# Where the modulation products of a two-block transformer stand in TensorE's order, and which tokens its first mixer takes first

## The chip, the cores and the metric

The kernel runs on one core of one Trainium2 chip, in one launch. The metric is the device time of that launch in microseconds (us). Three timed runs of the kernel before took 2777.68, 2779.40 and 2786.29 us; their median is 2779.4 us. The profiled execution is a run of its own.

The engines have short names in the rows: PE is TensorE (PEld its weight loads), DVE is VectorE, ACT is ScalarE, POOL is GpSimd and SP is SyncE, which issues most of the loads from HBM.

## What is computed

A first block of two layers (each a hybrid of sparse attention and a state space model, then a gated feed-forward) works on 256 tokens `x` of width 1024. A second block of two layers takes these as latent tokens together with 256 context tokens. Its layers are modulated: a conditioning vector is multiplied with `w_ada`, and the six resulting rows per layer shift, scale and gate the tokens. Cut to what matters here:

```python
def second_block(x, c, ctx, c_ctx, w_ada, b_ada, ...):      # x is the first block's normed output
    x_lat, x_ctx = x, ctx
    silu_c, silu_cc = jax.nn.silu(c), jax.nn.silu(c_ctx)
    for l in range(DEPTH):                                  # DEPTH = 2
        mod_l = (silu_c @ w_ada[l] + b_ada[l])              # w_ada[l]: 1024 x 6144, float32
        mod_c = (silu_cc @ w_ada[l] + b_ada[l])
        sh1, sc1, g1, sh2, sc2, g2 = jnp.split(mod_l, 6, axis=-1)
        h_l = rmsnorm(x_lat, norm_mix[l]) * (1 + sc1) + sh1
        h_c = rmsnorm(x_ctx, norm_mix[l]) * (1 + sc1c) + sh1c
        o_c, o_l = mixer(h_c, h_l, ...)                     # projections, attention, output projection
        x_lat = x_lat + g1 * o_l
        ...                                                 # sh2, sc2, g2: router and experts
```

`w_ada` depends on nothing that the first block computes, so its products may stand anywhere before the rows that they give are read.

## The kernel before

**Weights.** A float32 weight matrix is streamed in tiles of 128 x 4 x 512 into a ring of four slots (`g.ring`, one tile is 1 MB). `wtiles` (line 140) loads a tile on SP, splits each half of it into a high part (ScalarE, line 158) and a low part (VectorE, line 159), and the users (`lin_a`, `lin_a4`, `lin_b` and others) make three matmuls of each: high by high, high by low, low by high. `lin_a4` (line 181) keeps the split tiles and uses them for two groups of token tiles, one group after the other; `HALVES` is tiles 0 and 1 (latent), then 2 and 3 (context).

**Modulation units.** `ada_units` (line 923) is a generator. Each `next` of it, called through `g.filler`, makes one unit: one load of 1 MB of `w_ada` into a ring slot (line 945) and the products of it into the one PSUM bank `adaps` (line 947). Eight units make a group, six groups (two layers by three) make 48 units. At the end of a group VectorE adds the bias out of the bank (line 951), for two groups of three also a factor (line 955), GpSimd writes the rows to `g.mod` in HBM (line 957), and the next group begins with a bias load on SP into a tile with one buffer (line 941).

Units are drawn in these places:

- `wtiles` draws one at every eighth weight tile (`g.count % 8`, line 152). A layer of the first block takes 88 tiles, the mixer 14.
- `burst(g, n)` (line 307) draws n, each of whose matmuls must stand behind the last product so far (`g.last`). There are bursts of 3 and 4 in each layer of the first block (ahead of its two norms), of 5 at the start of the first mixer, and of 48 in the router, which takes what is left.

**The seam.** The first block ends with `final_norm` (line 800) of `x`, after the last tile of `ffn_w_down` (lines 174 to 176). The first mixer, `mixer_ab` (line 1158), then modulates all four token tiles in `mod_all` (line 1011): root mean square (line 982), two VectorE instructions per tile (lines 993 and 994), transposes and splits (`transpose_split`, lines 1005 to 1008). The context tokens `xc` were loaded after layer 0. The tiles `mh` that hold a modulated token tile have two buffers. Three `lin_a4` follow (lines 1249 to 1251), whose results go through norms and rotary products (`ev_x`, `ev_y`, `ev_z`), then low-rank products, then `attend` (line 1030): for each of eight pairs of heads scores, softmax, transposes and, in `values` (line 1079), the value products. The output projection and the router come behind it.

**What sets the order.** Each engine takes its instructions in an order that is fixed ahead of the run by a planner, which goes by the order of the program and by estimated times; an instruction that is not ready holds up what stands behind it on its engine. SP's order is fixed in the same way, over all loads.

Of the kernel before, what the change touches and what calls it, by code (L numbers as in the profile page):

```python
# [139 lines left out]
def wtiles(g, w2d, ktiles, pieces):  # L140

    nc = g.nc
    n = sum(p[1] for p in pieces)
    for k0 in range(0, ktiles, 4):
        kk = min(4, ktiles - k0)
        t = g.ring.tile([P, 4, 512], F32, name="wraw", tag="wraw")
        at = 0
        for c0, w in pieces:
            nc.sync.dma_start(t[:, :kk, at:at + w], w2d[k0 * P:(k0 + kk) * P, c0:c0 + w].rearrange("(k p) n -> p k n", p=P))
            at += w  # L150
        g.count += 1
        if g.count % 8 == 0:
            g.filler()
        for j in range(0, kk, 2):
            jj = min(2, kk - j)
            hi = g.split.tile([P, 2, 512], F32R, name="whi", tag="whi")
            lo = g.split.tile([P, 2, 512], F32R, name="wlo", tag="wlo")
            nc.scalar.copy(hi[:, :jj, :n], t[:, j:j + jj, :n])  # L158
            nc.vector.tensor_tensor(lo[:, :jj, :n], t[:, j:j + jj, :n], hi[:, :jj, :n].bitcast(F32), op=OP.subtract)  # L159
            yield k0 + j, jj, hi, lo  # L160
# [146 lines left out]
def burst(g, n):  # L307

    if g.last is None:
        for _ in range(n):  # L310
            g.filler()
        return
    with g.tc.issue_after(g.last.ins):
        for _ in range(n):
            g.filler()
# [516 lines left out]
Q_LORA, KV_LORA = 384, 256  # L832
HALVES = (range(2), range(2, 4))
O2_KR, O2_GQ, O2_GK, O2_GV = 640, 672, 1184, 1312
# [152 lines left out]
def modulated(g, pool, rows, tiles, rs=None):  # L987

    nc = g.nc
    rs = rs or rms_all(g, pool, tiles)  # L990
    for (r, y), (x, m) in zip(rs, tiles):
        a, b = rows[m]
        nc.vector.scalar_tensor_tensor(y, x, r, a, op0=OP.mult, op1=OP.mult)
        nc.vector.tensor_tensor(y, y, b, op=OP.add)
        yield y
# [12 lines left out]
        nc.vector.tensor_tensor(xl[:, k0:k0 + kk, t * P:(t + 1) * P], ps[:, :kk], a.bitcast(F32), op=OP.subtract)  # L1008


def mod_all(g, pool, l, xt, xh, xl):
    for i in (0, 2):
        for t, y in enumerate(modulated(g, pool, g.rows, xt[i:i + 2])):
            transpose_split(g, y, 8, xh, xl, i + t)

# [14 lines left out]
def attend(g, pool, pairs, qtiles):  # L1030


    nc = g.nc
    nt = len(qtiles)
    units = [(i, e, j) for i in range(len(pairs)) for e in range(2) for j in range(nt)]
    probs, pts, ready, biases = {}, {}, [], {}
    groups = []
    for j, (t, s0, ns) in enumerate(qtiles):
        if groups and groups[-1][2:] == [s0, ns]:
            groups[-1][1] = j + 1  # L1040
        else:
            groups.append([j, j + 1, s0, ns])

    def fetch(u):
        i, e, j = u
        if pairs[i][5] is not None:
            biases[u] = pairs[i][5](e, qtiles[j][0])

    def front(u):
        i, e, j = u  # L1050
        t, s0, ns = qtiles[j]
        n = ns * P
        ps = g.acc.tile([P, 512], F32, name="accps", tag="acc")
        nc.tensor.matmul(ps[:, :n], pairs[i][0](e, t), pairs[i][1](e, s0 * P, n), start=True, stop=True)
        if u in biases:
            nc.vector.tensor_tensor(ps[:, :S], ps[:, :S], biases.pop(u), op=OP.add)
        mx = pool.tile([P, 1], F32, name="smx", tag="smx", bufs=6)
        sm = pool.tile([P, 1], F32, name="ssm", tag="ssm", bufs=6)
        p = pool.tile([P, 512], F32, name="smp", tag="smp", bufs=5)
        nc.vector.tensor_reduce(mx, ps[:, :n], axis=AX.X, op=OP.max, negate=True)  # L1060
        nc.scalar.activation(p[:, :n], ps[:, :n], AF.Exp, bias=mx, accum_out=sm)
        nc.vector.reciprocal(sm, sm)
        nc.vector.tensor_scalar(p[:, :n], p[:, :n], sm, None, op0=OP.mult)
        probs[u] = p

    def back(u):
        i, e, j = u
        t, s0, ns = qtiles[j]
        if j == 0:
            pts[i, e] = pool.tile([P, 4, nt * P], F32, name="apT", tag="apT", bufs=3)  # L1070
        p, pT = probs.pop(u), pts[i, e]
        pt = g.aux.tile([P, 4, P], F32, name="auxps", tag="aux")
        for s_ in range(ns):
            nc.tensor.transpose(pt[:, s_, :], p[:, s_ * P:(s_ + 1) * P], g.ident)
        nc.scalar.copy(pT[:, s0:s0 + ns, j * P:(j + 1) * P], pt[:, :ns])
        if e == 1 and j == nt - 1:
            ready.append(i)

    def values(i):
        vf, o_hi, o_lo = pairs[i][2:5]  # L1080
        po = g.aux.tile([P, 512], F32, name="auxps", tag="aux")
        for j0, j1, s0, ns in groups:
            for s_ in range(s0, s0 + ns):
                for e in range(2):
                    nc.tensor.matmul(po[64 * e:64 * e + 64, j0 * P:j1 * P], vf(e, s_), pts[i, e][:, s_, j0 * P:j1 * P],
                                     start=(s_ == s0), stop=(s_ == s0 + ns - 1))
        nc.scalar.copy(o_hi, po[:, :nt * P])
        nc.vector.tensor_tensor(o_lo, po[:, :nt * P], o_hi.bitcast(F32), op=OP.subtract)

    lag, early = 3, 4  # L1090
    for u in units[:early]:
        fetch(u)
    for k in range(len(units) + lag + 1):
        if k + early < len(units):
            fetch(units[k + early])
        if k < len(units):
            front(units[k])
        todo = ready[:]
        ready.clear()
        if lag <= k < len(units) + lag:  # L1100
            back(units[k - lag])
        for i in todo:
            values(i)


def out_proj(g, pool, l, oh, ol, w2d, xt):
# [51 lines left out]
def mixer_ab(g, xt):  # L1158
    nc, tc, h = g.nc, g.tc, g.h
    with ExitStack() as st:  # L1160
# [11 lines left out]
        w_in = h["ab_w_in"]  # L1172
        with ExitStack() as s1:
# [7 lines left out]
            with ExitStack() as s2:  # L1181
                p2 = s2.enter_context(tc.tile_pool(name="mab2", bufs=1, side="right"))
                xh = p2.tile([P, 8, 512], F32R, name="mxh")
                xl = p2.tile([P, 8, 512], F32R, name="mxl")
                with tc.tile_pool(name="mabn", bufs=1) as pn:
                    burst(g, 5)
                    mod_all(g, pn, 0, xt, xh, xl)
                p3 = s2.enter_context(tc.tile_pool(name="mab3", bufs=1))
                qnr = p3.tile([P, Q_LORA], F32, name="qnr")
                knr = p3.tile([P, KV_LORA], F32, name="knr")  # L1190
# [55 lines left out]
                        nc.tensor.transpose(pt[:, j, :], v[:, 2 * j:2 * j + 2].rearrange("p a d -> p (a d)"), g.ident)  # L1246
                    nc.scalar.activation(qbT[:, :, t * P:(t + 1) * P], pt, AF.Copy, scale=0.125)

                lin_a4(g, xh, xl, w_in, 8, [(0, Q_LORA), (O2_GK, 128)], HALVES, ev_x)
                lin_a4(g, xh, xl, w_in, 8, [(Q_LORA, KV_LORA), (O2_GV, 128), (O2_KR, 32)], HALVES, ev_y)  # L1250
                lin_a4(g, xh, xl, w_in, 8, [(O2_GQ, 512)], HALVES, ev_z)
            pq = right.enter_context(tc.tile_pool(name="mabq", bufs=1, side="right"))
            qT = pq.tile([P, 8, 512], F32, name="qT2")
            kT = pq.tile([P, 8, 512], F32, name="kT2")
# [626 lines left out]
```

## Time and profile before

| | us |
|---|---|
| median of 3 runs | 2779.4 |
| profiled execution, time | 2780.57 |
| its span | 2778.8 |
| TensorE busy in the span | 2604.0 (94%) |
| VectorE busy | 1542.2 (55%) |
| ScalarE busy | 1024.1 (37%) |
| first block | 0 to about 1203 |
| first mixer, up to its attention | about 1203 to 1320 |
| its attention | about 1320 to 1430 |

A row of the order of instructions gives start, duration, engine, line, operation, tile written, tile read and count; in brackets stands the idle time of the engine just before it and what ended that. Matmuls overlap, so the price of one is read from start to start. A multiplication of float32 operands shows as two records.

### The profile page before, as it was taken

To read this page: it belongs to the slowest core of one execution; us is meant where nothing else is said; L and a number is where in the kernel's file an instruction comes from. 1 tells how busy PE (TensorE), PEld (TensorE's weight loads), DVE (VectorE), ACT (ScalarE), POOL (GpSimd) and SP (SyncE) were. 2 spreads that over 40 slices of the span, in tenths; PEclk is the share of its full clock that TensorE was granted. 3 is DMA by queue.
4 is the path that set the end of the run, shared out by engine and by line. 5 is a ranking of instruction groups with operands and counts; after the bars stand their busy time and mean duration, and the time that the engine had idled before them with its cause. 6 is when DMAs were issued, how large, how long until landed. Compare 5 with 4: busy or idle time off the path is not lost. (4 is left out here: it accounts for less than half of the span.)

```text
span 2778.8 us, 39439 instructions
## 1 busy us (share of the span) xinstructions
PE 2604.0 (94%) x15773; PEld 1840.4 (66%) x15773; DVE 1542.2 (55%) x2878; ACT 1024.1 (37%) x1809; POOL 131.0 (5%) x172
## 2 busy tenths in 40 slices
PE   7999999999999999988997999999989989998897
PEld 5889889977899889867665455445458554333332
DVE  6767768857777668655655434334363654222223
ACT  4556546634566456533652111111122441111011
POOL 0000000000000000011002000000000420000000
PEclk9999999999999999999997999999989889999999
DMA  6544457675455486662133999999933258999996
GB/s 220 196 152 152 150 201 234 202 240 179 136 175 171 150 287 193 203 208 68 54 153 124 402 420 420 420 420 419 385 122 112 92 209 346 420 420 420 420 420 284
DMA packets 207434, 694.56 MB, mean 250 GB/s; under 512 B 18160, under 2 KB 67760, under 8 KB 151184
## 3 DMA queue, kind: packets, MB, share of 16 engines
q1 hardware_dynamic: 201424, 674.18, 64.3%
q0 software_dynamic: 5824, 17.82, 2.0%
q8 instruction: 126, 2.06, 0.3%
q14 instruction: 60, 0.49, 0.1%
HBM read 690.80 MB, written 1.15 MB: 249 GB/s over the span
## 5 line engine op out<-in xcount | busy, mean ns | idle before, releaser
L159 DVE TENSOR_TENSOR wlo<-wraw,whi 128x1024 fp32r<-128x1024 f32 (+1 forms) x406 | 484.9, 1200 | 219.3 <-ACT whi L158 210.5
L158 ACT CAST whi<-wraw 128x1024 fp32r<-128x1024 f32 (+1 forms) x406 | 418.0, 1035 | 392.0 <-PE accps L245 195.4
L1657 PE MATMUL accps<-wraw,xg 128*64 128x512 f32 x2080 | 489.0, 595 | 40.8 <-DMA wraw<-in_moe_w_up 25.6
L1657 PEld LDWEIGHTS accps<-wraw,xg 128*64 128x64 f32 x2080 | 165.2, 138 | 354.6 <-issue 259.5
L244 PE MATMUL accps<-xh,whi 128*128 128x256 f32 x896 | 257.4, 287 | 0.0
L246 PE MATMUL accps<-xh,wlo 128*128 128x256 f32 x896 | 255.0, 285 | 0.0
L245 PE MATMUL accps<-xl,whi 128*128 128x256 f32 x896 | 254.6, 284 | 0.0
L1670 PE MATMUL accps<-wraw,eaT 128*64 128x512 f32 (+1 forms) x1040 | 234.2, 595 | 1.5 <-ACT eaT L1558 1.5
L1539 DVE TENSOR_TENSOR cmt<-auxps,g2r 128x512 f32<-128x512 f32 x108 | 73.6, 688 | 263.8 <-PE auxps L1537 263.2
L244 PE MATMUL accps<-fxh,whi 128*128 128x256 f32 x704 | 200.6, 285 | 0.8 <-ACT whi L158 0.8
L246 PE MATMUL accps<-fxh,wlo 128*128 128x256 f32 x704 | 199.6, 284 | 0.7 <-DVE wlo L159 0.5
L245 PE MATMUL accps<-fxl,whi 128*128 128x256 f32 x704 | 199.8, 284 | 0.0
L244 PEld LDWEIGHTS accps<-xh,whi 128*128 128x128 f32 x896 | 169.6, 189 | 7.7 <-issue 7.4
L246 PEld LDWEIGHTS accps<-xh,wlo 128*128 128x128 f32 x896 | 169.7, 189 | 1.1 <-issue 1.0
L245 PEld LDWEIGHTS accps<-xl,whi 128*128 128x128 f32 x896 | 169.5, 189 | 1.2 <-issue 1.0
L1558 ACT COPY eaT<-auxps 128x512 f32<-128x512 f32 x33 | 19.4, 586 | 408.7 <-PE auxps L1557 408.7
L1670 PEld LDWEIGHTS accps<-wraw,eaT 128*64 128x64 f32 (+1 forms) x1040 | 74.6, 137 | 133.2 <-issue 129.3
L244 PEld LDWEIGHTS accps<-fxh,whi 128*128 128x128 f32 x704 | 135.6, 193 | 6.3 <-issue 4.2
L246 PEld LDWEIGHTS accps<-fxh,wlo 128*128 128x128 f32 x704 | 135.5, 193 | 1.2 <-DVE wlo L159 1.2
L245 PEld LDWEIGHTS accps<-fxl,whi 128*128 128x128 f32 x704 | 135.8, 193 | 0.0
L1567 DVE TENSOR_TENSOR yl<-accps,yh 128x512 fp32r<-128x512 f32 x66 | 45.6, 692 | 161.3 <-ACT yh L1566 161.1
L1566 ACT CAST yh<-accps 128x512 fp32r<-128x512 f32 x66 | 38.6, 585 | 201.7 <-PE accps L1670 201.7
(496 smaller groups left out, 5139.2 us busy)
## 6 DMA issues: line engine op xcount, KB each, us to landing
wraw<-in_moe_w_gate SPq DMA_DIRECT2D x130, 1024.0 KB, 17.3
wraw<-in_moe_w_up SPq DMA_DIRECT2D x130, 1024.0 KB, 17.3
wraw<-in_moe_w_down SPq DMA_DIRECT2D x130, 1024.0 KB, 15.3
wraw<-in_w_in SPq DMA_DIRECT2D x72, 1024.0 KB, 5.1
wraw<-in_w_ada SPq DMA_DIRECT2D x48, 1024.0 KB, 4.9
wraw<-in_ffn_w_up SPq DMA_DIRECT2D x88, 512.0 KB, 5.0
wraw<-in_ffn_w_down SPq DMA_DIRECT2D x20, 1024.0 KB, 5.3
wraw<-in_w_proj_ssd SPq DMA_DIRECT2D x16, 1024.0 KB, 5.1
```

Source lines behind the costliest of these rows:

```text
L158: nc.scalar.copy(hi[:, :jj, :n], t[:, j:j + jj, :n])
L159: nc.vector.tensor_tensor(lo[:, :jj, :n], t[:, j:j + jj, :n], hi[:, :jj, :n].bitcast(F32), op=OP.subtract)
L244: nc.tensor.matmul(o, wh, a, start=(K == 0 and f % per == 0), stop=False, skip_group_check=True)
L245: nc.tensor.matmul(o, wh, b, start=False, stop=False, skip_group_check=True)
L246: nc.tensor.matmul(o, wl, a, start=False, stop=last, skip_group_check=True)
L1539: nc.vector.tensor_tensor(tm, ps, g2r[m][:, sl], op=OP.mult)
L1558: nc.scalar.copy(aT, ps)
L1566: nc.scalar.copy(yh[:, sl], psd[c])
L1567: nc.vector.tensor_tensor(yl[:, sl], psd[c], yh[:, sl].bitcast(F32), op=OP.subtract)
L1657: nc.tensor.matmul(pp[rows], xg[kh][:, k, cols], wt[:, k], start=(K == 0), stop=(K == 7))
L1670: nc.tensor.matmul(psd[c][rows], aT[:, k, rows], wt[:, 2 * kk + c], start=(k == 0), stop=(k == 3))
```

## The change

Four edits:

- `wtiles` draws a unit at every 20th weight tile instead of every eighth.
- `mod_all` takes the order of the token pairs as an argument, and the first mixer gives (2, 0): context tiles first, then latent tiles. The three `lin_a4` of the projections take the halves in reversed order, context first.
- A burst of two units stands behind each of these three projections.
- In `attend`, a unit is drawn after the value products of each pair (the second layer's mixer calls the same function, when no unit is left).

```diff
@@ wtiles
         g.count += 1
-        if g.count % 8 == 0:
+        if g.count % 20 == 0:
             g.filler()
@@
-def mod_all(g, pool, l, xt, xh, xl):
-    for i in (0, 2):
+def mod_all(g, pool, l, xt, xh, xl, first=(0, 2)):
+    for i in first:
         for t, y in enumerate(modulated(g, pool, g.rows, xt[i:i + 2])):
             transpose_split(g, y, 8, xh, xl, i + t)
@@ attend
         for i in todo:
             values(i)
+            g.filler()
@@ mixer_ab
                     burst(g, 5)
-                    mod_all(g, pn, 0, xt, xh, xl)
+
+                    mod_all(g, pn, 0, xt, xh, xl, (2, 0))
@@ mixer_ab
-                lin_a4(g, xh, xl, w_in, 8, [(0, Q_LORA), (O2_GK, 128)], HALVES, ev_x)
-                lin_a4(g, xh, xl, w_in, 8, [(Q_LORA, KV_LORA), (O2_GV, 128), (O2_KR, 32)], HALVES, ev_y)
-                lin_a4(g, xh, xl, w_in, 8, [(O2_GQ, 512)], HALVES, ev_z)
+                lin_a4(g, xh, xl, w_in, 8, [(0, Q_LORA), (O2_GK, 128)], HALVES[::-1], ev_x)
+                burst(g, 2)
+                lin_a4(g, xh, xl, w_in, 8, [(Q_LORA, KV_LORA), (O2_GV, 128), (O2_KR, 32)], HALVES[::-1], ev_y)
+                burst(g, 2)
+                lin_a4(g, xh, xl, w_in, 8, [(O2_GQ, 512)], HALVES[::-1], ev_z)
+                burst(g, 2)
```

## Rows read from the trace of the kernel before

**Rows 1.** The page: the span, and the loads of the modulation weights

```profile
span 2778.8 us, 39439 instructions
...
wraw<-in_w_ada SPq DMA_DIRECT2D x48, 1024.0 KB, 4.9
```

**Rows 2.** Stages: us; busy PE, PEld, DVE, ACT, POOL; clock; DMA share; GB/s

```profile
425.00:600.00 175.00, 175.00 (x1253) 163.08 (x1252) 135.89 (x228) 99.99 (x148) 1.76 (x3) 1.00 0.67 214
...
1203.00:1260.00 57.00, 42.61 (x220) 32.24 (x220) 40.05 (x82) 23.60 (x44) 14.79 (x22) 0.88 0.59 189
1260.00:1320.00 60.00, 53.08 (x250) 43.02 (x249) 31.96 (x70) 22.09 (x36) 9.54 (x8) 0.97 0.20 63
1320.00:1430.00 110.00, 109.33 (x579) 64.90 (x579) 72.76 (x207) 75.60 (x207) 3.64 (x6) 1.00 0.13 45
1212.00:1224.00 12.00, 6.46 (x23) 5.42 (x24) 9.96 (x12) 8.06 (x12) 1.00 (x3) 0.50 0.92 299
```

**Rows 3.** TensorE in order of time, a unit in the first block's stream

```profile
422.59 0.28 PE L245 MATMUL accps<-fxl,whi 128*128 128x256 f32 x1
422.71 0.28 PE L246 MATMUL accps<-fxh,wlo 128*128 128x256 f32 x1
422.92 1.06 PE L947 MATMUL adaps<-wraw,ccs 128*32 128x512 f32 x8
...
424.14 0.28 PE L245 MATMUL accps<-fxl,whi 128*128 128x256 f32 x1
```

**Rows 4.** TensorE in order of time, a burst of four in layer 0

```profile
406.69 3.64 PE L947 MATMUL adaps<-wraw,ccs 128*32 128x512 f32 x32
410.26 0.44 PE L292 MATMUL auxps<-cst,xn 128*128 128x128 f32 x2
```

**Rows 5.** TensorE in order of time, the start of the first mixer

```profile
1203.15 3.64 PE L947 MATMUL adaps<-wraw,ccs 128*32 128x512 f32 x32
1209.56 1.07 PE L947 MATMUL adaps<-wraw,ccs 128*32 128x512 f32 x8 [2.77 <-DVE badat L951]
1216.15 2.79 PE L1005 MATMUL auxps<-cst,mh 128*128 128x128 f32 x12 [5.53 <-DVE mh L994]
1220.33 0.77 PE L199 MATMUL accps<-whi,mxh 128*128 128x512 f32 x1 [1.39 <-ACT mxh L1007]
...
1234.48 0.39 PE L200 MATMUL accps<-wlo,mxh 128*128 128x512 f32 x1
1234.71 0.39 PE L201 MATMUL accps<-whi,mxl 128*128 128x512 f32 x1
```

**Rows 6.** VectorE, then ScalarE in order of time, at the same place

```profile
1207.62 1.28 DVE L808 SCALAR_TENSOR_TENSOR x<-x,fr,fnw 128x1024 f32<-128x1024 f32 x1 [0.66 <-POOL fr L130]
...
1212.39 2.48 DVE L993 SCALAR_TENSOR_TENSOR mh<-x,mr,ma 128x1024 f32<-128x1024 f32 x2 [2.12 <-POOL mr L130]
1214.78 2.35 DVE L994 TENSOR_TENSOR mh<-mh,mb 128x1024 f32<-128x1024 f32 x2
...
1212.26 1.99 ACT L158 CAST whi<-wraw 128x1024 fp32r<-128x1024 f32 x2 [2.17 <-DMA wraw<-in_ab_w_in]
1217.71 1.99 ACT L158 CAST whi<-wraw 128x1024 fp32r<-128x1024 f32 x2 [3.46 <-DMA wraw<-in_ab_w_in]
```

**Rows 7.** TensorE's waits by releaser, 1203 to 1320: us in all, times, longest

```profile
PE auxps L1246 <- DVE hnv L1214: 3.1, 2, 1.7
PE auxps L1226 <- DVE kdup L1223: 2.9, 2, 1.8
...
PE auxps L1246 <- DVE hnv L1027: 2.5, 1, 2.5
```

**Rows 8.** SP: a wait by releaser (us, times, longest), and issues in order

```profile
SPq L941 <- DMA mod<-badat: 8.6, 1, 8.6
...
1205.13 4.40 SPq L149 DMA_DIRECT2D wraw<-in_ab_w_in  x5
```

**Rows 9.** TensorE in order of time, a pair's value products in the attention

```profile
1406.40 2.81 PE L1085 MATMUL auxps<-apT,vb 128*64 128x256 f32 x24
```

## The prediction

> **What bounds the kernel now.** I read the busy time of the engines by stage first [rows 2], since a mean over the span says nothing of one stage. In the first block's stream TensorE is busy for 175.00 of 175 us: it alone sets the pace, VectorE (135.89) and ScalarE (99.99) have slack, and the DMA share is 0.67. In the attention of the first mixer TensorE is busy for 109.33 of 110 us at full clock, with a DMA share of 0.13. Between the two lies the only slack the change can use: TensorE is busy for 42.61 of 57 us and then for 53.08 of 60 us, so 21.3 us are idle. The order of TensorE's instructions shows where [rows 5]: 2.77, 5.53 and 1.39 us at the start of the mixer, before the first product of the projections at 1220.33; the waits by releaser show the longest of the rest, 3.1, 2.9 and 2.5 us for results of VectorE that are to be transposed [rows 7]. Everything that the change touches is therefore priced in TensorE time: full price where it has no idle time, less where it has.
>
> **The modulation unit.** A unit is one load of 1 MB into a slot of the weight ring and eight matmul records. The load lands in 4.9 us [rows 1] and hides behind other work in a saturated stage. On TensorE, single in the stream, the start-to-start step of the neighbours is 0.12 us (422.59 to 422.71); from 422.71 to 424.14 lie two such steps and a unit, so the unit costs 1.43 - 0.24 = 1.19 us [rows 3]. Four in a bunch take from 406.69 to 410.26, so 0.89 us each [rows 4].
>
> **Counting.** Each layer of the first block draws 88 weight tiles, the mixer 14. Before, 176/8 = 22 units stand in the first block's stream, 14 in its four bursts, 5 in the burst at the mixer's start, 1 in the mixer's stream (tile 184), 6 in the router: 48. After, 176/20 = 8 stand in the stream, 14 and 5 as before, 1 in the mixer's stream (tile 180), 6 in the three new pairs, 8 in the attention, 6 in the router. So 14 leave the stream, 6 go behind the projections and 8 into the attention. The router's number does not change, in spite of the title.
>
> **1. Removed from the stream: -16.7 us.** 14 x 1.19. The stream has no idle time that could swallow it, and their 14 loads go from a queue that is not the bound.
>
> **2. Added to the attention: +8.8 us.** There is no wait to fill (109.33 of 110), so each of the 8 is paid in full: between 8 x 0.89 = 7.1 and 8 x 1.19 = 9.5. I take 1.1 each, nearer to the single one, since each stands alone behind a pair's value products [rows 9]. Those products are themselves 64-column tiles, so the switch may be a little cheaper than in the stream. The switch is what makes a single unit dearer than a bunched one: 0.30 us by rows 3 and 4. The Trainium skill (TensorEngine Tiling, Key Properties) says that changing the tiling mode drains TensorE, which speaks against spreading units singly; by that rule all 8 cost 1.19 and the term is 9.5, and by the bunched row it would be 7.1.
>
> **3. Six units behind the projections: +2.7 us.** In pairs they cost 6 x 0.89 = 5.3 us if nothing hides them. They stand behind the last product of a projection, where the transposes of the norms wait, and the three longest kinds of such waits sum to 8.5 us [rows 7]. But these waits come a few products later, in an order fixed ahead of the run, so a unit that runs earlier may only push the wait back. Ends 0 and 5.3; I take the middle. The single one in the mixer's stream is the same before and after.
>
> **4. Context tokens first: -7 us.** Before, TensorE goes idle at 1206.7, when four units are done, because the chain of the latent tokens starts only with the final norm: two products of 1.28 us (L808, the second from 1207.62 to 1208.9), squares and roots, then from 1212.39 on 2.48 and 2.35 us of modulation on VectorE [rows 6], and the first transpose at 1216.15 [rows 5]. The context tokens need none of the final norm; they need room that the last products of the first block hold until about 1203.2. If their modulation runs ahead of the final norm's products, their first transposes come at about 1203.2 + 3.5 (squares and roots, as from 1208.9 to 1212.39) + 2.48 + half of 2.35 = 1210.4; if behind them, at 1208.9 + 2.48 + 1.2 = 1212.6. From the first transpose to the first product it takes 4.2 us before (1216.15 to 1220.33), less at full clock. The weights are the other limit: the first tile's cast starts at 1212.26, on its landing, and takes half of 1.99 [rows 6]. So products start at 1213.3 at best and at 1216.8 at worst, against 1220.33: a gain of 3.5 to 7.0. The second weight tile is cast from 1217.71 [rows 6]; the 24 products on the first tile at 0.23 us (1234.48 to 1234.71) [rows 5] take 5.5 us, so TensorE comes to it at 1218.8 and hardly waits. The latent tokens then have 11 us of context products as cover for their own norm and modulation. What is late next: VectorE, 40.05 busy of 57 [rows 2], which splits weights, modulates and subtracts for both halves at once. With that comes the clock: from 1212 to 1224 the granted clock is 0.50 (1.2 GHz) after the idle 5.53 us, and TensorE's 6.46 us of work there would have taken half at 2.4 GHz [rows 2], so 0 to 3.2 us come back. I take 5.5 and 1.5. The Trainium skill (TensorE: Matmul & The Clock Gate, Part 1) says that the clock falls after an idle TensorE and returns with sustained work; the row agrees. By that rule, if the context transposes break up the idle time, the whole 3.2 comes back and the term is -8.7; if not, -5.5.
>
> **5. The unit count shifts the group ends: +1.3 us.** After every eighth unit VectorE adds the bias out of the one PSUM bank, and the ninth unit waits for it, as it does for 2.77 us at 1209.56 [rows 5]. Before, one burst holds such an end (unit 40). After, unit 8 falls into the burst ahead of the first feed-forward, where the four units now end just when the transposes can begin (410.26) [rows 4], and unit 24 into the mixer's, where it replaces the one of before. So between 0 and 2.77 us are new; I take 1.3. Behind the waiting unit in TensorE's order stand that norm's transposes, and on SP the next bias load, which waits for the write-back (8.6 us in the mixer) with weight loads behind it [rows 8].
>
> **Edits at nothing.** Reversing the halves in the three projections moves no work; rotary products of the latent tokens now come last, with products of the next projection over them. The attention's 8 loads take ring slots ahead of the four loads of the output projection, which are issued ahead of the attention now; by the ring's turn three of their four slots come free before the last pair, and a load lands in 4.9 us [rows 1]. GpSimd's writes of the modulation rows are off TensorE's path. All that follows (experts, second layer) shifts with the router's end.
>
> **Sum.** -16.7 + 8.8 + 2.7 - 7.0 + 1.3 = -10.9 us. The profiled run took 2780.57 us (span 2778.8 [rows 1] and 1.8 around it), 1.2 above the median of 2779.4; off the median the forecast is 2768.5 us. With every term at its good end: -16.7 + 7.1 + 0 - 10.2 + 0 = -19.8; with every term at its bad end and nothing from part 4: -16.7 + 9.5 + 5.3 + 0 + 2.8 = +0.9.
>
> **Rivals.**
> *The weight loads come late.* SP takes its instructions in order. The bias load behind unit 24 waits for a write-back; before, five loads of the first weights passed ahead of it (from 1205.13, 4.40 us), then it held SP for 8.6 us, to about 1218.2 [rows 8]. If it now stands ahead of them, the first weights are issued then and, with the 7.1 us from 1205.13 to 1212.26 and a cast, the first product starts at about 1226.3, 6 later than before: -16.7 + 8.8 + 2.7 + 6.0 + 1.3 = +2.1, so 2781.5. Against it: the order of before let weights pass. Chance 0.08.
> *Only the place changes.* VectorE takes the final norm first and the splits between, the latent half comes late again, and the pairs hide nothing: -16.7 + 8.8 + 5.3 + 1.3 and a gain of 0 to -2 give about -2, so 2777. For it: VectorE is the busiest engine there. Chance 0.13.
> *Every wait is filled.* The waits of rows 7 and the whole start close: -16 to -19.8, so 2761. Chance 0.17.
> *Slower: units in the attention wait for their loads.* Before, no transfer is needed on TensorE's path there. A unit whose 1 MB is not there stops TensorE and with it the scores and transposes queued behind it for up to 4.9 us [rows 1]. Four slots run ahead; if the later four units each wait for a whole load, 4 x 4.9 = 19.6 us come on top of -10.9: +8.7, so 2788. It decides from a mean wait of 1.4 us over the 8 units, above which the gain is gone. Against it: the pairs lie some 13 us apart (109 us for 8), far over 4.9. Chance 0.06.
>
> **How the numbers follow.** The forecast has 0.56, with its own range of 2763 to 2774. About 0.3% (8.3 us) is what a measurement of this kernel can tell from no change, so faster begins below 2771.1: 0.45 of the 0.56 lies there and 0.11 above. Faster 0.45 + 0.17 = 0.62; same 0.11 + 0.13 + 0.05 of the late loads = 0.29; slower 0.03 + 0.06 = 0.09. The range of 2760 to 2777 takes in the filled waits and the upper part of "only the place changes", and leaves out the late loads and the slower case.
>
> **What would show it.** In the profile of the changed kernel: the burst at the mixer's start, now at 1203.15 [rows 5], near 1187.8 (16.7 less 1.3 earlier); from there to the first projection product 10 to 13 us instead of 17; the attention longer by 7 to 10 us with no idle row ahead of a unit; six units in the projections with less than 8.5 us left in the waits of rows 7. Wrong would be: a stream that is not shorter by 1.19 per unit, idle time ahead of a unit in the attention, SP held by the bias load ahead of the mixer's weights, or later stages that do not shift by the same time.

## The result, and the profile after

The changed kernel takes 2799.33 us in the median of 10 runs (2791.07 to 2802.09), the kernel before beside it 2780.41 (10 runs, 2777.68 to 2790.87). The ratio is 1.0052, with a 95% interval of 1.0038 to 1.0067: it is slower, where the forecast was 2768.5 and at most 2777. A second series of the same kernel gave 1.0059 [1.0046, 1.0072] (e12 below).

The page of the profiled execution of the kernel after: the span and the first of the engines' busy times.

```profile
span 2799.3 us, 39440 instructions
...
PE 2627.0 (94%) x15773; PEld 1855.5 (66%) x15773; DVE 1540.0 (55%) x2878; ACT 1024.1 (37%) x1809; POOL 131.0 (5%) x172
```

The number of TensorE's instructions is that of before (15773), so nothing was added; 23 us of busy time were (2604.0 before). The stages that answer to [rows 2], with the same columns:

```profile
425.00:600.00 175.00, 175.00 (x1260) 164.26 (x1259) 135.16 (x226) 101.90 (x150) 0.59 (x1) 1.00 0.65 215
1206.00:1263.00 57.00, 46.62 (x225) 31.67 (x225) 39.53 (x81) 22.71 (x44) 15.08 (x22) 0.88 0.66 221
1263.00:1323.00 60.00, 53.30 (x261) 40.20 (x260) 28.34 (x68) 15.75 (x32) 10.75 (x10) 0.97 0.43 149
1336.00:1450.00 114.00, 113.20 (x570) 58.97 (x570) 66.25 (x194) 71.52 (x196) 4.81 (x8) 1.00 0.27 92
```

The stages look alike; what differs is where they lie. The start of the first mixer, TensorE in order of time, the lines that answer to [rows 5]:

```profile
1206.03 1.93 PE L947 MATMUL adaps<-wraw,ccs 128*32 128x512 f32 x16
1210.56 4.48 PE L947 MATMUL adaps<-wraw,ccs 128*32 128x512 f32 x24 [2.61 <-DVE badat L951]
1215.65 1.06 PE L1005 MATMUL auxps<-cst,mh 128*128 128x128 f32 x8 [0.60 <-DVE mh L994]
1219.47 0.80 PE L199 MATMUL accps<-whi,mxh 128*128 128x512 f32 x1 [2.76 <-ACT whi L158]
```

The burst stands at 1206.03, where 1187.8 was forecast and 1203.15 was before: 14 units have left the stream, and in this execution the first block is not shorter but 2.9 us longer. From the burst to the first product of a projection it takes 13.44 us instead of 17.18. The wait of 5.53 us for the modulated tile is 0.60 now, the group's end stays (2.61), and the cast of the first weights is what comes last (2.76).

The account by marks that both kernels have, all from TensorE in order of time:

| from, to | before, us | after, us | difference | forecast |
|---|---|---|---|---|
| start of the program to the mixer's burst | 1203.15 | 1206.03 | +2.9 | -15.4 |
| burst to the first projection product | 17.18 | 13.44 | -3.7 | -5.5 |
| first projection product to the first score (L1054) | 115.4 | 126.1 | +10.7 | +1.2 (pairs 2.7, clock -1.5) |
| first score to the output projection (attention) | 96.7 | 113.9 | +17.2 | +8.8 |
| output projection to the first gather product (L1605, after: L1610) | 85.3 | 82.7 | -2.6 | 0 |
| the rest of the span | 1261.0 | 1257.1 | -3.9 | 0 |
| sum | 2778.8 | 2799.3 | +20.5 | -10.9 |

Three rows carry the result: a stream that did not get shorter (18.3 us off the forecast), projections that got longer (9.5 off, taken apart by e2 and e7 below), and an attention that got longer by twice the forecast (8.4 off). The first of the three is not the same in the second profile of this kernel (e12). The attention first. TensorE in order of time there, a pair of the kernel after:

```profile
1396.84 1.05 PE L947 MATMUL adaps<-wraw,ccs 128*32 128x512 f32 x2
1397.82 0.66 PE L1074 MATMUL auxps<-cst,smp 128*128 128x128 f32 x4
1398.40 1.95 PE L1085 MATMUL auxps<-apT,va 128*64 128x256 f32 x16
1399.75 1.47 PE L1085 MATMUL auxps<-apT,va 128*64 128x256 f32 x12
1401.14 1.06 PE L947 MATMUL adaps<-wraw,ccs 128*32 128x512 f32 x6
1402.13 1.12 PE L1054 MATMUL accps<-kbT,qbT 64*128 64x512 f32 x2
```

One unit stands there as two pieces: two records (one product of 32 columns) ahead of the value products, six (the other three) behind them. The piece of two takes from 1396.84 to 1397.82, 0.98 us; the piece of six from 1401.14 to 1402.13, 0.99 us. A whole unit of eight takes 0.99 to 1.0 us by the same reading in the first block. So a piece costs what a whole unit costs, and the eight units of the attention are paid for twice: their sixteen pieces take 15.7 of the 17.2 us. Nothing waits for a load: no row ahead of a unit shows idle time.

Now the stream. In the records of the granted clock (1.0 is 2.4 GHz, 0.5 is 1.2) I added up the stretches at half rate between 30 and 1200 us, that is, in the first block behind its cold start: 17.0 us in five stretches before, 61.3 us in twelve after. Work at half rate takes nearly twice as long (two neighbouring products of the first projection start 0.43 us apart at half rate, 1221.32 to 1221.75, and 0.23 at full rate [rows 5]), so the block lost up to 44.3 / 2 = 22.2 us more: without that, it is 19.3 us shorter (1203.15 - 8.5 against 1206.03 - 30.7), more than the 16.7 forecast. Four of the places, by windows of about the same work (after, then before; us, busy PE, PEld, DVE, ACT, POOL, clock, DMA share, GB/s):

```profile
145.00:155.00 10.00, 8.28 (x25) 5.42 (x26) 5.32 (x11) 3.43 (x7) 0.00 (x0) 0.66 0.57 198
223.00:230.00 7.00, 6.47 (x41) 6.27 (x41) 5.74 (x12) 3.45 (x8) 0.70 (x1) 0.76 0.12 24
267.00:274.00 7.00, 6.55 (x43) 6.34 (x43) 4.06 (x7) 3.22 (x6) 0.70 (x1) 0.76 0.01 2
615.00:632.00 17.00, 16.80 (x73) 15.01 (x72) 10.88 (x33) 8.36 (x16) 0.00 (x0) 0.60 0.90 318
```

```profile
145.00:155.00 10.00, 6.62 (x24) 4.21 (x25) 6.61 (x14) 5.62 (x14) 0.00 (x0) 0.83 0.66 210
223.00:230.00 7.00, 6.47 (x55) 6.27 (x55) 5.01 (x10) 3.35 (x8) 0.70 (x1) 1.00 0.12 42
267.00:274.00 7.00, 6.55 (x54) 6.34 (x55) 4.16 (x8) 3.47 (x7) 0.70 (x1) 1.00 0.00 0
615.00:632.00 17.00, 16.80 (x99) 14.32 (x98) 15.44 (x46) 10.91 (x19) 0.00 (x0) 1.00 0.95 343
```

TensorE is busy in these windows to within 0.1 us of before (but for the first); in the same busy time it gets fewer products done, 41 records instead of 55, at a clock of 0.76 instead of 1.00. This is why a share of busy time shows nothing of it. Three of the stretches come on at a wait: the softmax's, which ends at 146.7 us (3.62 us, 2.97 before), and the norm's in the scan at 224 and 269 (0.53 and 0.45 us, as long as before). The fourth begins at 617, some 3 us behind waits of 0.64 and 0.55 us.

### The profile page after: what moved, and what is told of

The parts are those of the page before. It is cut to its first block, busy times and chain, and to the rows that moved or that the text cites. A ratio compares the mean times of both kernels' runs of the same rounds, so it can differ in the third digit from the quotient of the medians.

```text
span 2799.3 us, 39440 instructions
## 1 busy us (share of the span) xinstructions
PE 2627.0 (94%) x15773; PEld 1855.5 (66%) x15773; DVE 1540.0 (55%) x2878; ACT 1024.1 (37%) x1809; POOL 131.0 (5%) x172
```

## The experiments

A quantity of its own separates what an edit does to the work from what the clock does. For each execution the span and the mean granted clock are known; span times clock is the time at full rate, and the span less that is what the clock took. (It is a split of the same time, not a law: a wait does not get shorter at full rate.) Span times clock varies with a standard deviation of 1 to 3 us from run to run and the mean of a series is good to about 1 us, so a difference of two means to about 2, while the spans of a kernel go up and down with the clock's part (correlation 0.8 to 0.97 in nearly all series). The clock's part varies by 4 to 8 us from run to run in most series, and a difference of two of its means is known to about 5 us. Means over each series:

| kernel | ratio to before, 95% | span x clock | taken by the clock |
|---|---|---|---|
| before (33, 23 and 23 runs) | 1 | 2704.3, 2704.4, 2704.8 | 79.1, 77.9, 77.4 |
| after (10 runs; e12, 5 runs) | 1.0052; 1.0059 | 2711.4; 2710.0 | 84.4; 87.9 |
| e1, stream thinned, 14 units out | 0.9967 [0.9951, 0.9983] | 2684.3 | 90.5 |
| e2, context first alone | 0.9990 [0.9976, 1.0004] | 2706.4 | 74.4 |
| e3, after with whole units in attention | 1.0006 [0.9994, 1.0019] | 2699.9 | 84.0 |
| e4, after without the attention's units | 0.9996 [0.9982, 1.0009] | 2690.4 | 90.6 |
| e5, as e1 at other places | 0.9934 [0.9919, 0.9949] | 2682.7 | 82.0 |
| e6, before at other places | 0.9996 [0.9986, 1.0006] | 2701.2 | 80.4 |
| e7, e3 without the pairs | 0.9990 [0.9975, 1.0005] | 2695.5 | 83.9 |
| e8, a unit in every 11th tile, pairs, without the attention's eight | 1.0053 [1.0038, 1.0068] | 2713.6 | 82.5 |
| e9, e7's order, places of e5, rest in the router | 1.0018 [1.0009, 1.0027] | 2704.5 | 82.9 |
| e10, before with 14 units moved behind the attention | 1.0093 [1.0079, 1.0108] | 2711.0 | 97.6 |
| e11, e3 at the places of e5 | 0.9972 [0.9963, 0.9981] | 2697.0 | 77.0 |

**e1_stream_out**: term 1 alone.

```
-        if g.count % 8 == 0:
+        if g.count % 20 == 0:
...
-            for k in range(8):
+            nk = 8 if l == 0 else (4, 3, 3)[gr]
+            for k in range(nk):
```

> The kernel before, with one unit per 20 weight tiles instead of one per eight; the 14 units that leave the first block's stream are left out of the program (second layer's products with 4, 3 and 3 of 8 parts of w_ada), nothing is put elsewhere. Theory A (a unit in the stream costs 1.19 us, and what the changed kernel lost there it lost to the granted clock): span times mean granted clock falls from 2704.7 us to about 2688, wherever the clock lands; at the clock of before (0.973) the time is about 2763, at 0.968 about 2778. Theory B (the stream was not bound by TensorE, so that removing units gives nothing): span times clock stays within 4 us of 2705, and the mixer starts within 4 us of 1203 with no more half-clock time than before.

2777.55 us against 2785.25. The work got shorter by 20.0 us (2704.3 to 2684.3), 1.43 per unit, and the clock took 11.4 us more (79.1 to 90.5). In its profile the first projection product stands at 1220.35, that of before at 1220.33. So taking 14 units out of a saturated stream, and putting them nowhere, is worth 0.33%: at these places, this was the whole room that the change had (e5 below takes others).

**e2_ctx_first**: term 4 alone, in the kernel before.

```
-                    mod_all(g, pn, 0, xt, xh, xl)
+                    mod_all(g, pn, 0, xt, xh, xl, (2, 0))
...
-                lin_a4(g, xh, xl, w_in, 8, [(0, Q_LORA), (O2_GK, 128)], HALVES, ev_x)
+                lin_a4(g, xh, xl, w_in, 8, [(0, Q_LORA), (O2_GK, 128)], HALVES[::-1], ev_x)
```

(and so for the two other projections)

> The kernel before with the context tokens first in the first mixer (modulation and the three projections) and nothing else. Theory A (the edit shortens only the idle time at the start, and VectorE gives part of it back in the first projection): from the burst at the mixer's start to the first projection product 13.4 us instead of 17.2, span times clock 0 to 4 us below 2704.7. Theory B (it costs: the latent half's long norm now comes last and holds the projections): span times clock 2 to 6 us above 2704.7.

From the burst to the first product it takes 10.34 us (1210.94 to 1221.28) instead of 17.18, the upper end of the forecast's gain. But from there to the first low-rank product it takes 85.5 us instead of 82.5, and from that to the first score 35.0 instead of 32.9: 5.1 of the 6.8 us are given back. TensorE in order of time:

```profile
1221.28 0.79 PE L199 MATMUL accps<-whi,mxh 128*128 128x512 f32 x1 [1.23 <-ACT whi L158]
...
1226.58 1.85 PE L1005 MATMUL auxps<-cst,mh 128*128 128x128 f32 x12 [1.18 <-DVE mh L994]
1229.45 0.50 PE L199 MATMUL accps<-whi,mxh 128*128 128x512 f32 x1 [1.01 <-ACT mxh L1007]
...
1314.29 0.76 PE L268 MATMUL accps<-cqh,whi 128*128 128x512 f32 x1 [2.01 <-DVE hnv L1213]
1322.61 0.50 PE L268 MATMUL accps<-cqh,whi 128*128 128x512 f32 x1 [1.10 <-DVE qT L1259]
```

The latent half is late still, only behind the context half. Twelve of its transposes (1.85 us), which stood ahead of the first product before, stand behind it now, and TensorE stops for its modulation and eviction in the midst of the projections (1.18, 1.01). The waits at the low-rank products, which take all the tokens (2.01, 1.10), are not new: there were 1.45 and 1.68 us for the same norms before. From the first product to the first score the waits over 0.4 us sum to 13.7 us here and to 11.4 before. So 1.85 of the 5.1 us are work that has only changed sides of the mark, 2.3 are new waits, and 0.9 are not accounted for. By the whole span the order is worth 0.1%, which this measurement can't tell from nothing (+2.1 us of work, 4.7 less to the clock).

**e3_units_whole**: the changed kernel with each attention unit tied behind the last value product of its pair.

```
-                    nc.tensor.matmul(po[64 * e:64 * e + 64, j0 * P:j1 * P]
+                    g.last = nc.tensor.matmul(po[64 * e:64 * e + 64, j0 * P:j1 * P]
...
             values(i)
-            g.filler()
+            burst(g, 1)
```

> The changed kernel, with each unit of the attention tied behind its pair's last value product, so that its four products stay together. Theory A (the planner cut each unit in two, one product ahead of the value products and three behind, and each piece costs as much as a whole unit): the attention, first score to first output product, falls from 113.9 us to about 105.5, span times clock from 2710.1 to about 2702. Theory B (the unit's price in the attention is set by who stands beside it, not by the cut): the attention stays above 111.

The same place in the attention, TensorE in order of time:

```profile
1405.23 2.81 PE L1085 MATMUL auxps<-apT,vb 128*64 128x256 f32 x24
1407.97 1.07 PE L947 MATMUL adaps<-wraw,ccs 128*32 128x512 f32 x8
1408.97 0.66 PE L1074 MATMUL auxps<-cst,smp 128*128 128x128 f32 x4
```

The unit is one piece of 1.00 us, and the attention takes 103.7 us instead of 113.9. The ratio falls from 1.0052 to 1.0006, and the work by 11.5 us. Two lines that keep a unit's four products together are worth nearly the whole loss.

**e4_attention_out**: the changed kernel without the attention's units.

```
             values(i)
-            g.filler()
...
+            nk = 8 if l == 0 else (6, 5, 5)[gr]
```

> The changed kernel without units in the attention; these 8 are left out of the program (second layer's products with 6, 5 and 5 of 8 parts of w_ada). Theory A (each cut unit costs 2.15 us): the attention falls from 113.9 to 96.7 us as before, span times clock from 2710.1 to about 2693. Theory B (part of the 17 us belongs to the reversed order of the tokens or to the loads): the attention stays at 100 us or above.

The attention is back at 96.7 us. Against e3 this prices the eight whole units: 7.0 us in the stage (103.7 - 96.7), 9.5 in the mean work of the whole program. Each unit of e3 takes 1.00 us from its start to that of the next product. The last one stands ahead of the output projection, where TensorE waits for a cast, and shortens that wait from 1.63 to 0.63 us: seven units are paid in the stage and one is hidden. TensorE in order of time, e4, then e3:

```profile
1433.81 1.20 PE L199 MATMUL accps<-whi,oh 128*128 128x512 f32 x4 [1.63 <-ACT whi L158]
```

```profile
1431.57 1.07 PE L947 MATMUL adaps<-wraw,ccs 128*32 128x512 f32 x8
1433.27 1.20 PE L199 MATMUL accps<-whi,oh 128*128 128x512 f32 x4 [0.63 <-ACT whi L158]
```

The time hardly moves (0.9996 against 1.0006), since the clock took 6.6 us more.

**e7_pairs_out**: e3 without the three pairs behind the projections.

```
-                burst(g, 2)
```

(three times, and six units of the second layer left out)

> The changed kernel with the attention units kept whole (as e3_units_whole) and without the three pairs behind the first mixer's projections; six units are left out of the second layer's modulation. Prices term 3 by its own kernel. If the pairs cost what their rows show beside the waits they fill (8.6 us of pieces, 1.5 us of waits filled): from the end of the first projection to the first low-rank product 53 us instead of 60.5, span times clock 2693 (7 below e3's 2700), median 2779. If they are hidden as forecast (2.7): span times clock 2697, median 2784. Attention 103 to 105 us as in e3.

From the first projection product to the first low-rank product it takes 86.3 us instead of e3's 94.2, from there to the first score 35.2 instead of 33.0: the six units cost 5.7 us in the stages and 4.4 in the mean work. A wait of 2.01 us among the low-rank products (1301.72) is there and in e3 is not. From the first product to the first score the waits over 0.4 us sum to 12.8 us here and to 10.7 in e3, so the pairs fill about 2 us. With the 5.1 us of e2, the 5.7 make up the 10.7 by which the projections got longer.

**e5_stream_out_other_places** and **e6_same_units_other_places**: number of units or places?

```
e5, in e1:              g.count % 20 == 0  ->  g.count % 20 == 10
e6, in the kernel before: g.count % 8 == 0  ->  g.count % 8 == 4
```

> The kernel before with a product unit in every 20th weight tile of the stream, as in e1_stream_out, but started at the 10th tile instead of the 20th, so that the nine units stand at other places; 14 units are left out of the second layer's modulation, so less work is done than the reference asks. Question: does the first block lose clock because fewer units are in its stream, or because of where they happen to stand? Theory A (fewer units: TensorE reaches the waits of the first block earlier, waits longer there, and the half-rate stretches get more): as e1, span times mean granted clock 2684 +-4, time lost to the clock 88 to 92 us, median 2775 to 2780. Rival B (place only: e1 and the changed kernel stand badly): lost 76 to 82 us, median 2763 to 2768.

> The kernel before, all its work, with the unit after every 8th weight tile started at the 4th instead of the 8th: as many units in the stream, at other places. Theory A (the number of units decides what the clock loses): lost 77 to 81 us as before (79), span times clock 2704 to 2709, because the planner cuts six of the units in two here, and a cut unit costs a unit more where the parts are far apart (up to +6); median 2783 to 2790. Rival B (the places decide): lost 85 to 92, median 2790 to 2798, or under 74 and a median below 2779.

e5 does e1's work (2682.7 and 2684.3), but the clock takes 82.0 instead of 90.5, and the ratio is 0.9934 instead of 0.9967: both the clock's part and the median (2767.14) lie within rival B's bounds, at their edge. e6 keeps to theory A in the clock's part (80.4) though its one profile shows 47.6 us at half rate in the first block, against 17.0 of before. So the number of units in the stream does not set what the clock takes. The shift moves one unit besides: e5 has nine of them in the first block and one in the output projection, e1 eight and one in the mixer's projections. Nor do the places in the stream settle it alone: e3 and e4 have the same, and there the clock takes 84.0 and 90.6. The cut units of e6 did not cost the 6 us that I had allowed: its work is 3 us below that of before.

**e12_changed_again**: the changed kernel itself, for a second profile.

> The changed kernel itself, for a second profile and more executions beside the same kernel before as the others. If the first profile's half-rate stretches in the first block (some 61 us of them after the first 30 us, where the kernel before had 17) belong to the kernel, this profile shows 50 us or more of them again, at the same waits (the softmax's, the core's), and lost 82 to 88 us; if they were one execution's, under 35 us and lost near 79. Span times clock 2711 +-3, ratio 1.004 to 1.007.

The windows of about the same work as above, 3 us earlier here:

```profile
142.00:152.00 10.00, 6.81 (x19) 4.22 (x20) 5.63 (x12) 4.90 (x13) 0.00 (x0) 0.66 0.65 211
220.00:227.00 7.00, 6.47 (x43) 6.27 (x43) 4.39 (x8) 2.84 (x7) 0.70 (x1) 0.76 0.16 61
264.00:271.00 7.00, 6.56 (x44) 6.20 (x44) 3.65 (x6) 2.85 (x7) 0.70 (x1) 0.76 0.01 2
612.00:629.00 17.00, 16.47 (x98) 14.12 (x99) 15.48 (x47) 10.65 (x19) 0.00 (x0) 1.00 0.99 363
```

40.8 us at half rate between 30 and 1200 us, between the two numbers set ahead. In this profile the mixer's burst stands at 1194.01, 9.1 us earlier than before and not 2.9 later, while the three stages behind it take 13.45, 127.8 and 113.9 us, as in the first profile (13.44, 126.1, 113.9). The falls at the softmax and in the scan are there again at the same instructions (0.66, 0.76, 0.76), so these belong to the program; the long one at 615 us is not (1.00 instead of 0.60), so that one was chance. The first profile thus overstates the clock's part; over the runs it is 5.3 us (84.4 against 79.1) to 10.5 us (87.9 against 77.4).

**e8_pairs_only, e9_whole_units_rest_in_router, e10_rest_in_router**: all the work, at cheaper places, as I thought.

```
e8, in the changed kernel:  no g.filler() in attention;  g.count % 11 == 0
e9, in e3:                  no burst(g, 2);              g.count % 20 == 10
e10, in the kernel before:  g.count % 20 == 10
```

> All the work, none in attention: the changed kernel with a unit in every 11th tile of the stream (16 there) and without the attention's eight; the six that leave the stream stand in the pairs behind the projections. By the runs so far a unit in the stream costs 1.43 us clock-free (20.0/14), one in a pair 0.67 ((2690.4-2684.3-2.1)/6), and the context first costs 2.1: span times clock 2704.3 - 8.6 + 4.0 + 2.1 = 2701.8. Theory A (clock loss grows with the units taken out of the stream, 11.4 us for 14, and the context first gives 4.7 back): lost 79.3, median 2781, no change. Rival (the clock doesn't follow the number): lost 74, median 2776, faster by 0.3%.

> All the work of the reference. Stream units at the places of e5_stream_out_other_places (nine, from the 10th tile on, every 20th), the context first, eight whole units in attention, no pairs: the six others stand in the router's burst. By the prices so far: span times clock 2682.7 (e5) + 2.1 (context first) + 9.5 (eight whole units in attention) + 6 units at 0.91 (the burst's row, 3.64 us for four) 5.5 = 2699.8; lost to the clock 78 to 84: median 2779 to 2785, no change against before. If the router's waits hide its units: 2694 and 2774 to 2779.

> All the work. The kernel before with nine units in its stream instead of 22 (places of e5) and nothing else: the other 14 stand in the router's burst, where TensorE is idle for a large part of the stage before the experts. If TensorE's rows or the arrival of the units' weights set the burst's end: 14 units at 0.91 = 12.7 and three ends of groups at up to 2.8 more: span times clock 2682.7 + 13 to 21 = 2696 to 2704, median 2778 to 2787. If the router's waits hide them: 2683 to 2687, median 2766 to 2770, faster by 0.5%.

All three miss, and all to the slow side. In e8 the work is 2713.6 where 2701.8 was reckoned. Two kinds of rows in its stream speak of why: six units are cut (mostly into two records and six, 0.98 and 0.99 us), and two find their weights not there (1.24 and 1.27 us):

```profile
144.95 1.07 PE L947 MATMUL adaps<-wraw,ccs 128*32 128x512 f32 x8 [1.24 <-DMA wraw<-in_w_ada]
...
843.07 1.04 PE L947 MATMUL adaps<-wraw,ccs 128*32 128x512 f32 x2
844.37 1.06 PE L947 MATMUL adaps<-wraw,ccs 128*32 128x512 f32 x6
```

A seventh unit, drawn in the output projection, stands cut near the end of the attention, which takes 97.7 us instead of 96.7; a wait of 0.62 us (at 1426.69 before) is gone there. Six pieces more in the stream and two waits come to 8.4 us of the 11.8; since e6's cut units cost nothing that shows, this is an account and no proof. In e10 the stage from the output projection to the first gather takes 122.1 us instead of e5's 83.7, 2.7 us for each of the 14 units, where I had reckoned with 0.91. TensorE's waits by what ended them, 1470 to 1550 us (us in all, times, longest):

```profile
PE adaps L947 <- DMA wraw<-in_w_ada: 15.3, 13, 3.5
```

A unit needs 1 MB, and in the router's burst they follow each other faster than they land. TensorE is idle there, but a unit is a transfer first. e9 pays the same with six units: 95.6 us in that stage, e11 79.0.

**e11_whole_units_pairs**: the best of the parts.

```
in e3:  g.count % 20 == 0  ->  g.count % 20 == 10
```

> All the work. The changed kernel with its attention units whole (e3_units_whole) and its nine stream units at the places of e5. By the prices: 2682.7 + 2.1 + 9.5 + 4.4 (the pairs, e3 against e7) = 2698.7; lost 78 to 84 where e3 lost 84: median 2778 to 2784. If the places alone made e5 faster than e1 (lost 82 against 90.5), this one is 6 to 8 us below e3's 2786.5 against the same kernel before; if that was chance, it is at e3's ratio, 1.0006.

2776.08 us (12 runs) against 2784.48: 0.9972 [0.9963, 0.9981], faster than both kernels: by 0.28% against the one before, and by 0.9% against the changed one in the same series (2800.89). The work (2697.0) is as reckoned. The clock takes 77.0 where e3 lost 84.0, a step of 7.0 us by the same shift of places that gave 8.5 from e1 to e5.

## Why the prediction was wrong, step by step

Three steps failed: that a unit in the attention stays in one piece (term 2, the largest), that nothing in a saturated stream can swallow a saving (term 1), and that the latent half is covered by the context products (term 4).

**What bounds the kernel** held. The first block and the attention are TensorE's alone, and the units there were paid in full but for the one that e3 hides.

**Term 1 (stream, -16.7).** The size was low: 20.0 us of work left, 1.43 per unit instead of the 1.19 read off [rows 3]. Where the other 0.24 us per unit come from no run shows. What failed is the sentence that the stream has no idle time that could swallow it. The clock could: it took 11.4 us more in e1, 5.3 to 10.5 in the changed kernel (the 4.1 of e5 are within what such a difference is known to). I had priced the clock at the mixer's start alone, because [rows 2] show 1.00 in one window of the block; the stretches at half rate lie elsewhere, and I had not asked what would change them.

**Term 2 (attention, +8.8).** This is the largest error. Measured 17.2 in the stage, and by e4 and e3 in the mean work 9.5 for whole units and 11.5 for cutting them. The term took a unit to be one thing that stands behind a pair's value products. The code says only that the unit comes after them in the program; the order is made ahead of the run, product by product, and it put one of the unit's four products ahead of the value products. I read the unit's price from a row where it was whole and did not ask what keeps it whole: this call ties it to nothing, and e3, which ties it, gets it whole. Whole, the unit costs 1.00 us by its row, between the prices of [rows 4] and [rows 3]; so the price of a whole unit was near, and the unit was not whole. "No wait to fill" was not quite so either: the window read in [rows 2] ends at 1430, short of the wait of 1.63 us that hides one unit in e3. The Trainium skill (TensorEngine Tiling (Array Packing), Key Properties) says that a change of the tiling mode drains TensorE, which made me lean to 1.1. A single unit costs 0.11 us more here than one of a burst (0.89). The same section says that tiles operate independently and can run in parallel, and that is what the pieces show: one product alone takes 0.98 us, three together 0.99.

**Term 3 (pairs, +2.7, 0 to 5.3).** 4.4 by the mean work, 5.7 by the stages of e7 and e3: near the upper end. About 2 us of waits are filled, while the order cuts two of the three pairs around transposes (x10 and x6, x4 and x12), though a burst is tied behind an instruction, and pays for each piece. TensorE in order of time, the first pair after the first projection:

```profile
1253.70 1.90 PE L947 MATMUL adaps<-wraw,ccs 128*32 128x512 f32 x10
1255.53 0.55 PE L1005 MATMUL auxps<-cst,ly 128*128 128x128 f32 x3
1256.01 1.06 PE L947 MATMUL adaps<-wraw,ccs 128*32 128x512 f32 x6
```

Two units take 1.83 and 0.99 us here, 2.82 in all, against 1.78 by [rows 4]. The waits that were to hide them (2.65 and 2.84 us for hnv) came later, as the prediction had feared.

**Term 4 (context first, -7).** The start came early as forecast, 6.8 us in e2 and 3.7 in the changed kernel. The step that failed is the sentence on what is late next: I had the latent tokens' norm and modulation covered by 11 us of context products, and e2 shows two new waits for them, 2.2 us, and 1.85 us of their transposes behind the mark. I had priced the start of the chain, by the first product, and not its end, the low-rank products, which need both halves. In the mean work the order costs 2.1 us; with the clock's part it gains 2.6, both near what can be told from nothing. Of the 1.5 us of clock nothing shows in the two profiles: from the burst to the first score the mean granted clock is 0.94 before and 0.94 after. The reading of [rows 2] was off besides: the clock was at 0.50 from 1210.7 on (1.00 from 1209.0 to 1210.6), thus through the idle 5.53 us and not only after them.

**Term 5 (group ends, +1.3).** At the mixer the wait of before (2.77) is replaced by one of 2.61; at the other place no wait of such length appeared (0.42 us at 412.50). Nothing to be seen of it.

**The sum of the parts as measured**, in time at full clock: -20.0 (e1) + 2.1 (e2) + 4.4 (e3 less e7) + 9.5 (e3 less e4) + 11.5 (after less e3) = +7.5; the changed kernel itself has +7.1 (2711.4 less 2704.3). The clock's 5.3 us come on top: 12.4 in all, 0.45%, inside the interval of the ratio. Each of the five parts is good to about 2 us, so that the two sums agree to 0.4 is luck.

**The rivals.** The late weights did not come: three loads of the first weights are issued from 1208.01 on, ahead of the bias load at 1218.72. The first product does wait 2.76 us for the first cast, but the row of that cast (1218.37) shows no wait for its load; ahead of it on ScalarE stand an eviction of context transposes (1216.36) and the squares of a latent tile (1217.32). The units in the attention did not wait for loads. "Only the place changes" was nearest in spirit, at 2777. The slower ending that came, a unit in pieces, was not among them.

**What stays open.** Why the clock took 8.5 and 7.0 us less after the shift of places (e1 to e5, e3 to e11) is not settled, nor that the places did it: the profiles of e5 and e11 show 47.6 and 34.0 us at half rate in the first block, those of e1 and e3 54.5 and 30.6, and single profiles vary by as much. Even the 17.0 us of the kernel before are one profile's: e2, whose stream has its units at the same places, shows 34.1, and has the long stretch near 615 us too (as do the first profile of the changed kernel, e1 and e9; the ten others do not). Nor is it shown why the falls in the scan come in the changed kernel and not before, where the waits are as long. They do go with the stream: all ten profiles of kernels with a unit in every 20th tile, and those of e6 and e8, have a fall at one or more of these waits of 0.40 to 0.55 us; the two with the units at the places of before (before and e2) have none.

## What to carry to other kernels

When filler work is a set of products that run side by side, look in the order of instructions whether the set stays together: here a piece costs as much as the whole. Tying the set behind an instruction kept it whole in the attention and did not in two of the three pairs, so look again after the edit. A filler also has to be fed: put it where its load has landed, not merely where the engine is idle. And when work is taken out of a saturated stream, compare the granted clock of the same work in both profiles, or span times clock over many runs, before the saving is believed.

## What the hardware showed that I had not expected

- One matmul record pair of 32 columns takes as long (0.98 us) as three such products together (0.99 us) or four (1.00 us).
- Behind waits of 0.45 to 0.53 us in a stream that is otherwise full, the granted clock fell to 0.5 in the changed kernel, in both its profiles, and stayed at 1.00 in the kernel before with waits of the same length (0.45 and 0.53). Twelve of fourteen profiles have such falls; the two without have the stream of the kernel before.
- In the same stretch of the changed kernel, one execution ran at a mean clock of 0.60 (615 to 632 us, TensorE busy for 16.80 of 17) and another at 1.00 (16.47 of 17). The Trainium skill (TensorE: Matmul & The Clock Gate, Part 1) says of the ramp at a kernel's start that it differs from run to run of one kernel; here a stretch in the middle does.
- The clock's part is worth 74 to 98 us of these kernels. Edits that left nearly all of the work alone went with changes of 6.6 to 11.4 us in it (before to e1, e1 to e5, e3 to e11, e3 to e4), each known to about 5 us.
